# A gated unit in two column blocks of 512 instead of four of 256

## The chip, the cores and the metric

The kernel runs on one core of a Trainium2 chip. The core has five engines that work side by side, each on its own queue of instructions in program order: TensorE (PE, matrix products into PSUM), VectorE (DVE), ScalarE (ACT), GpSimd (POOL) and SyncE (SP, which here issues the DMAs). PSUM has eight banks of 512 fp32 columns. The metric is the device time of one execution in microseconds, from the chip.

## The reference

One layer of a hybrid backbone for 1,024 latent tokens of width 1,024 with 256 context tokens. Its mixer is a bidirectional S5 scan, then GELU, then a gated unit, then a residual; a SwiGLU FFN with 2,816 hidden channels and a final norm follow. The part the change touches:

```
g = gelu(y)                                  # (1024 tokens, 1024 channels)
y = g * sigmoid(g @ w_glu + b_glu)           # w_glu is 1024 x 1024
x = x + gate_mix * y                         # gate from the adaLN row
h = rms_norm(x) * (1 + scale) + shift        # input of the FFN
x = x + gate_ffn * swiglu(h, w1, w3, w2)
```

## The kernel before

All products must keep fp32 accuracy. A matrix is split in a high part `h`, rounded to the fast fp32r format, and a low part `l`, the rest; a product is three matmuls, h·wH + h·wL + l·wH. ACT or DVE makes the high part (a copy that rounds), POOL or DVE the low part (a subtraction).

The program is one order written by hand (a manual schedule): each engine runs its instructions in the order of the text, and waits only for data and for buffers. Up to the gated unit this order stands in two strings of codes, `PROG1` and `PROG2`, which `run` reads. The codes of the end of `PROG2`:

- `Q`, `H`: state products and GELU of channel block k (eight blocks of 128 channels)
- `I`, `J`: for tokens of the first half, transpose block k on PE and copy it as the high part (ACT), then make the low part (DVE); `GH[0]` holds both. `GH[1]` is for the second half
- `w`, `l`: load pieces of `w_glu` (raw fp32) into the buffers `wr0` and `wraw`; `b` loads the bias
- `W`, `V`: split weights into high and low parts. `V` first takes over the region `ra`, which held the scan's states
- `g`: the first matmuls of the gated unit, for those channel blocks that are ready. `g03` is token tile 0 up to block 3
- `x`: gate (multiply by the adaLN row) four blocks of one token tile on POOL

A *unit* `(cq, s)` is column block `cq` of `w_glu` for token tile `s` (eight tiles of 128 tokens). `glu_unit` issues its matmuls (`glu_mm`, lines L1092 to L1094), then on DVE the bias add, on ACT the sigmoid, on DVE the product and the add of the residual row `xs` (which is read from DRAM again, four rows of 512 KB at L1110), and on ACT a square with row sums for the norm (L1129). Between these it takes one step of each generator handed to it.

Before, `w_glu` is cut in four column blocks of 256, so there are 32 units of 24 matmuls. Two loops run them. The first loop runs the four blocks for token tiles 0 to 3. Its first eight units also turn the second half's channel blocks (`gt_steps`: four transposes, ACT copy, DVE subtraction). Weight blocks 2 and 3 are split inside this loop. The second loop runs token tiles 4 to 7, sixteen units numbered `u`. Beside them it makes the FFN's input for tiles that are done: `rms_steps` (a row sum and a chain of some twelve tiny DVE operations, L1152 and on), `h2s_steps` (POOL scales both halves of a tile, issued at the last step of a unit), and `h2t_steps` (four transposes a half, scale and shift on ACT for the first half and DVE for the second, ACT copy, subtraction on POOL for the first half and DVE for the second). One half is turned in each unit. At unit 12 the first FFN weights are split (`op_split`, four ACT casts and four POOL subtractions), and after unit 15 the up projection (`up_plain`, L1281 to L1283) starts. It turns the last tile after 36 of its matmuls.

PSUM tiles of both loops come from a pool of eight banks (`pe8`), each handed out again in the order in which they came free.

Of the kernel before, what the change touches and what calls it, by code (L numbers as in the profile page):

```python
# [10 lines left out]
F32 = mybir.dt.float32  # L11
# [6 lines left out]
P = 128  # L18
D = 1024
# [13 lines left out]
PROG2 = ("T12 T13 T14 T15 Z0 N0 Z1 Z2 D0 Z3 N1 D1 Z4 H0 H1 N2 D2 H2 w0 w1 l1 N3 Z5 D3 H3 N4 D4 z6 z7 I0 J0 I1 J1 H4 N5 D5 I2 J2 H5 I3 J3 W0 W1 x0 x1 x2 x3"  # L33
         " Q6 H6 I4 J4 Q7 b0 I5 J5 H7 g03 g13 I6 J6 g23 g05 g15 I7 J7 V1 w20 w21 g26 x10 x11 x12 x13")
LOG2E = 1.4426950408889634
LN2H = 0.693359375
LN2L = -2.12194440e-4
# [5 lines left out]
def s5_ffn_kernel(tc, a, out):  # L43
# [3 lines left out]
    with ctx:  # L47
# [906 lines left out]
        def run(prog):  # L954


            for w in prog.split():
# [7 lines left out]
                elif op == "L":  # L965
                    cs_load(i, S)
                elif op == "G":
                    cs_sign(i)
                elif op == "B":
                    bb_put(1, bb_turn(1))  # L970
                    bb_put(0, bb_turn(0))
                elif op == "C":
                    q, part = divmod(i, 10)
                    for f in cl_ops(q, part, cts[q][part], HOW[q][part]):
                        f()
                elif op == "F":
                    fill(*divmod(i, 10), *((RW, 0) if i >= 30 else (RC[3], 12)))
                elif op == "T":
                    toeplitz(i)
                elif op == "R":  # L980
                    turned(i, 0, HSe[i], S)
                elif op == "Z":
                    turned(i, 1, HSl[i], ENG[ZEN[i]])
                elif op == "z":
                    turned(i, 2, HSq[i], ENG[ZEN[i]])
                elif op == "P":
                    inner[i] = x_mm(i, pw)
                    states_mm(i, inner[i], 0, HSe[i], False)
                elif op == "Q":
                    inner[i] = x_mm(i, pe8)  # L990
                    states_all(i, inner[i], HSq[i])
                elif op == "Y":
                    S.copy(yview(i // 2, i % 2), inner[i // 2][i % 2])
                elif op == "N":
                    late[i] = [pe8([4, T, HC]) for _ in range(2)]
                    states_mm(i, late[i], 1, HSl[i], True)
                elif op == "D":
                    for gp, po in enumerate(late[i]):
                        tt(yview(i, gp), po, yview(i, gp), ADD)
                elif op == "H":  # L1000
                    if i in late:
                        S.activation(Y[:, i], Y[:, i], AF.Gelu_apprx_tanh)
                    else:
                        for gp in range(2):
                            S.activation(yview(i, gp), inner[i][gp], AF.Gelu_apprx_tanh)
                elif op == "I":
                    if GH[0] is None:
                        GH[0] = tuple(view(region(t, 16, R32), 0, [4, 8, P]) for t in ("c1", "c0"))
                    late[i] = gt_hi(i, 0)
                elif op == "J":  # L1010
                    gt_lo(i, 0, late[i])
                elif op == "W":
                    if not WR:
                        W0.append(region("c2", 16, R32))
                        WR.append((view(W0[0], 0, [8 * 256]), view(W0[0], 8, [8 * 256])))
                    v = slice(1024 * i, 1024 * i + 1024)
                    split(wr0[i], (WR[0][0][:, v], WR[0][1][:, v]), E, V)
                elif op == "w":
                    cq, h = divmod(i, 10)
                    SY.dma_start(wr0[h], a["w_glu"][cq][:, 1024 * h:1024 * h + 1024])  # L1020
                elif op == "b":
                    SY.dma_start(bglu, a["b_glu"].to_broadcast([P, D]))
                elif op == "l":
                    load_glu(i)
# [12 lines left out]
        late, W0, WR, PZ, GH, GR = {}, [], [], {}, [None, None], []  # L1037
        wr0 = [view(RXa, 4, [1024]), view(RW, 0, [1024])]
        bglu = view(RU, 32, [D])
        wraw = view(RXc, 0, [2048])  # L1040

        def load_glu(cq):
            SY.dma_start(wraw, a["w_glu"][cq])
# [39 lines left out]
        def glu_mm(cq, s, ks):  # L1083

            wH, wL = (w.rearrange("p (k n) -> p k n", k=8) for w in WR[cq])
            h_, l_ = gh_(s)
            new = (cq, s) not in PZ
            if new:
                PZ[cq, s] = [pe8([256]), 0]
            pz, n = PZ[cq, s]  # L1090
            for k in ks[n:]:
                PE.matmul(pz, h_[:, k], wH[:, k], start=n == 0, stop=False)  # L1092
                PE.matmul(pz, h_[:, k], wL[:, k], start=False, stop=False)
                PE.matmul(pz, l_[:, k], wH[:, k], start=False, stop=n == 7)  # L1094
                n += 1
            PZ[cq, s][1] = n
            return pz

        HOW = [[{"P": PE, "Y": SY, "E": E, "V": V}[c] for c in h] for h in HOWS.split()]
# [8 lines left out]
        xs = [view(X1, 4 * i, [D]) for i in range(4)]  # L1108
        for s in range(4):
            SY.dma_start(xs[s], xr[:, s])  # L1110
        TT = [[view(GR, 32 + 16 * i + 8 * j, [4, 4, P]) for j in range(2)] for i in range(3)]
        def glu_unit(cq, s, *others):

            def step():
                for g in others:
                    next(g, None)

            cs_ = slice(cq * 256, cq * 256 + 256)
            pz = glu_mm(cq, s, range(8))
            step()  # L1120
            tt(pz, pz, bglu[:, cs_], ADD)
            S.activation(pz, pz, AF.Sigmoid)  # L1122
            step()
            y = Y[:, 2 * cq:2 * cq + 2, s]
            o = pz.rearrange("p (k n) -> p k n", k=2)
            tt(o, o, y, MUL)
            tt(y, o, xs[s % 4][:, cs_].rearrange("p (k n) -> p k n", k=2), ADD)
            step()
            S.activation(o, y, AF.Square, accum_out=ssq[:, s, cq:cq + 1])  # L1129
            step()  # L1130
# [18 lines left out]
        def rms_steps(s0, s1):  # L1149
            sl = slice(s0, s1)  # L1150
            yield
            V.tensor_reduce(ss2[:, sl], ssq[:, sl], AX.X, ADD)  # L1152
            rsqrt(rt[:, sl], ss2[:, sl], rtt[:, sl])
            yield

# [40 lines left out]
            SY.dma_start(wraw[:, 512 * a0:512 * a1], a["w13"][ft].rearrange("p w k n -> p (w k n)")[:, 512 * a0:512 * a1])  # L1196
# [68 lines left out]
        GB = [[view(g, kb + 4 * i, [D]) for i in range(4)] for g, kb in ((G2, 0), (GR, 32))]  # L1265

        def gb(ft):
            return GB[ft == NFT - 1]
# [445 lines left out]
def layouts(i):  # L1714
# [30 lines left out]
    a["w_glu"] = c(f["s5_w_glu"][0].reshape(8, P, 4, 256).transpose(2, 1, 0, 3).reshape(4, P, 2048))  # L1745
# [22 lines left out]
```

## Time and profile before

| | us |
|---|---|
| median of 3 runs | 1016.01 (1014.42 to 1016.13) |
| the profiled execution | 1015.21 |
| its span, first to last instruction | 1013.4 |
| first gated-unit matmul to first up matmul | 258.79 to 361.32 |

In the rows of the profile, a line of the table by stretches gives for each engine the busy us and, in brackets, how many instructions it ran in the stretch, then the clock granted to PE (1.00 is full) and the DMA share and GB/s. In a row in order of time stand start, duration, engine, line, operation, output <- inputs, shape, and in brackets the idle time before it with what ended it; x4 means four instructions in one row. In a group, `| 1.2, 1218 |` are busy us and mean ns of one. Matmuls are pipelined, so their pace is read from start to start and not from their duration. L77 is the helper that issues every two-operand elementwise instruction. Buffer names: `pe` is PSUM of this stage, `ru` holds the residual stream, `rxa`, `rw` and `rxc` are the raw buffers `wr0` and `wraw` point into, `c` and `ra` hold split operands.

### The profile page before, as it was taken

The page shows a single profiled execution, that of the slowest core. Times are in us where ns is not written, and L with a number is a line of the kernel's source. Part 1 is how long each engine was busy: PE and PEld are TensorE (multiplying, and loading weights), DVE is VectorE, ACT ScalarE, POOL GpSimd, SP SyncE. Part 2 cuts the span into 40 slices and gives each one's busy share as a digit, 9 for nine tenths or more (in the row PEclk, how much of TensorE's full clock was granted, in tenths as well). Part 3 has the DMA queues.
Part 4 walks back from the last instruction along what each step waited for, and adds up shares of the span by engine and source line. Part 5 has one row for each costly group of instructions (what it writes and reads, how often), then busy time and mean ns, then how long its engine had stood idle before and what let it go on. Part 6 is the DMA issues. An engine that isn't in the chain of part 4 may idle for free. (4 is left out here: it accounts for less than half of the span.)

```text
span 1013.4 us, 18560 instructions
## 1 busy us (share of the span) xinstructions
PE 959.4 (95%) x6988; PEld 772.1 (76%) x6988; DVE 780.4 (77%) x1638; ACT 438.9 (43%) x860; POOL 763.4 (75%) x590
## 2 busy tenths in 40 slices
PE   5988798779999999999999999999999999999996
PEld 1466523679999988778888888888888888888885
DVE  7989699996356867877958677686959677686987
ACT  5478622335444663443343343324343343324337
POOL 5799998994672448979785878777786878777764
PEclk9999999999999999999999999999999999999998
DMA  9765997334512021011212111121212111121205
GB/s 336 280 135 95 280 346 247 95 84 138 188 46 80 2 104 63 27 44 46 73 42 83 42 52 42 50 66 53 73 42 83 43 52 43 46 70 53 73 22 166
DMA packets 48546, 98.96 MB, mean 98 GB/s; under 512 B 4284, under 2 KB 18876, under 8 KB 47176
## 3 DMA queue, kind: packets, MB, share of 16 engines
q1 hardware_dynamic: 43272, 86.64, 26.0%
q0 software_dynamic: 2016, 7.34, 3.9%
q10 hardware_dynamic: 3168, 3.79, 1.1%
q8 instruction: 55, 0.90, 0.4%
q14 instruction: 35, 0.29, 0.1%
HBM read 84.25 MB, written 6.17 MB: 89 GB/s over the span
## 5 line engine op out<-in xcount | busy, mean ns | idle before, releaser
L77 POOL TENSOR_TENSOR c<-rxc,c 128x512 fp32r<-128x512 f32 x128 | 166.6, 1315 | 53.5 <-ACT c L1222 52.7
L1282 PE MATMUL ut<-ra,c 128*128 128x512 f32 x400 | 155.7, 389 | 1.2 <-DVE ra L77 1.2
L1281 PE MATMUL ut<-ra,c 128*128 128x512 f32 x400 | 155.7, 389 | 0.2 <-ACT ra L1222 0.2
L1283 PE MATMUL ut<-ra,c 128*128 128x512 f32 x400 | 155.6, 389 | 0.0
L1222 ACT CAST c<-rxc 128x512 fp32r<-128x512 f32 x128 | 79.1, 622 | 147.0 <-PE xt L1576 53.3
L1576 PE MATMUL xt<-c,c 128*128 128x512 f32 x540 | 129.7, 389 | 0.0
L1576 PEld LDWEIGHTS xt<-c,c 128*128 128x128 f32 x540 | 101.4, 188 | 21.0
L77 DVE TENSOR_TENSOR ru<-ru,xt 128x1024 f32<-128x1024 f32 x90 | 107.3, 1215 | 10.9 <-PE xt L1576 7.9
L77 DVE TENSOR_TENSOR ru<-ut,ru 128x512 f32<-128x512 f32 x98 | 67.2, 686 | 43.0 <-PE ut L1283 37.6
L1282 PEld LDWEIGHTS ut<-ra,c 128*128 128x128 f32 x400 | 75.1, 188 | 17.0 <-POOL rxc L77 1.5
L1281 PEld LDWEIGHTS ut<-ra,c 128*128 128x128 f32 x400 | 75.1, 188 | 16.1 <-ACT ra L1222 0.6
L1283 PEld LDWEIGHTS ut<-ra,c 128*128 128x128 f32 x400 | 75.1, 188 | 15.5
L77 POOL TENSOR_TENSOR c<-rw,c 128x512 fp32r<-128x512 f32 (+1 forms) x29 | 41.1, 1417 | 37.8 <-ACT c L1222 37.8
L77 POOL TENSOR_TENSOR c<-ru,c 128x512 fp32r<-128x512 f32 (+1 forms) x39 | 57.1, 1465 | 10.1 <-ACT c L1222 5.7
L1281 PE MATMUL ut<-c,c 128*128 128x512 f32 x160 | 62.3, 390 | 0.8 <-DVE rxa L77 0.8
L77 POOL TENSOR_TENSOR rxc<-rxc 128x512 f32<-128x512 f32 x40 | 61.4, 1535 | 1.6
L1282 PE MATMUL ut<-c,c 128*128 128x512 f32 x160 | 62.2, 389 | 0.0
L1283 PE MATMUL ut<-c,c 128*128 128x512 f32 x160 | 62.2, 389 | 0.0
L1576 PE MATMUL ut<-c,c 128*128 128x512 f32 x216 | 51.9, 389 | 0.0
L584 PE MATMUL pv<-ru,c 128*64 128x160 f32 x512 | 45.0, 316 | 5.6 <-ACT rxa L388 1.8
L77 DVE TENSOR_TENSOR pe<-pe,ru 128x256 f32<-128x256 f32 x64 | 27.4, 429 | 29.5 <-ACT pe L1122 17.4
L77 DVE TENSOR_TENSOR ru<-ru,ut 128x512 f32<-128x512 f32 x76 | 47.3, 680 | 0.3
(444 smaller groups left out, 2569.1 us busy)
## 6 DMA issues: line engine op xcount, KB each, us to landing
c<-in_ada_w SPq DMA_DIRECT2D x46, 256.0 KB
rxc<-in_w SPq DMA_DIRECT2D x38, 256.0 KB
rxc<-in_w SPq DMA_DIRECT2D x19, 512.0 KB
ru<-in_w SPq DMA_DIRECT2D x11, 512.0 KB
rw<-in_w SPq DMA_DIRECT2D x11, 512.0 KB
ra<-in_ada_w SPq DMA_DIRECT2D x10, 512.0 KB
ra<-in_ada_w SPq DMA_DIRECT2D x18, 256.0 KB
ru<-in_xT SPq DMA_DIRECT2D x4, 1024.0 KB
```

What stands on the lines that cost most here:

```text
L77: eng.tensor_tensor(out=o, in0=x, in1=y, op=op)
L584: PE.matmul(pv[64 * (i % 2):64 * (i % 2) + 64, ri, c0:c0 + 160], w[:, i, 64 * ri:64 * ri + 64], U[:, 8 * b + 4 * j + i], start=True, stop= ...
L1222: S.copy(o[0], x)
L1281: PE.matmul(pu, wh, bh, start=start, stop=False)
L1282: PE.matmul(pu, wh, bl, start=False, stop=False)
L1283: PE.matmul(pu, wl, bh, start=False, stop=stop)
L1576: PE.matmul(pd, w[:, cs_], b, start=j in (1, 2, 4) and n == 0, stop=n == 2, skip_group_check=j not in (1, 2, 4))
```

## The change

`w_glu` is cut in two column blocks of 512, so there are 16 units of 24 matmuls, each filling a whole PSUM bank. The order of work around them changes with it:

- The first block arrives in four raw quarters (`w0 w1` and the first `l1`), of which DVE makes the high parts (`W0` to `W3`). The low parts are made in `V1`, two on POOL and two on DVE, since they lie in region `ra`. Until then `g` codes multiply by the high weights alone (`glu_h`: h·wH and l·wH). Units (0, 0) to (0, 2) then start with nothing left but their eight products with the low weights.
- The second block's raw quarters (`w20 w21` and the second `l1`) are loaded into the same four buffers behind `V1`, and before the residual rows `xs` on SP's queue. They are split after units (0, 0) and (0, 1), two quarters each, high on ACT and low on POOL.
- The gates `x10` to `x13` move from the end of `PROG2` to after unit (0, 2).
- In the first loop all eight units turn a channel block; in the second, eight units each turn both halves of a tile. The norms run at u = 0, 4 and 6, and `op_split` at u = 6.

```diff
-PROG2 = ("T12 ... I3 J3 W0 W1 x0 x1 x2 x3"
-         " Q6 H6 I4 J4 Q7 b0 I5 J5 H7 g03 g13 I6 J6 g23 g05 g15 I7 J7 V1 w20 w21 g26 x10 x11 x12 x13")
+PROG2 = ("T12 ... I3 J3 W0 W1 W2 W3 x0 x1 x2 x3"
+         " Q6 H6 I4 J4 Q7 b0 I5 J5 H7 g03 g13 I6 J6 g23 g05 g15 I7 J7 V1 w20 w21 l1 g26")
...
                 elif op == "W":
-                    if not WR:
+                    if not W0:
                         W0.append(region("c2", 16, R32))
-                        WR.append((view(W0[0], 0, [8 * 256]), view(W0[0], 8, [8 * 256])))
-                    v = slice(1024 * i, 1024 * i + 1024)
-                    split(wr0[i], (WR[0][0][:, v], WR[0][1][:, v]), E, V)
+                        late["wh"] = view(W0[0], 0, [8, 512])
+                    V.tensor_copy(view(W0[0], 4 * i, [1024]), wr0[i])
...
                 elif op == "V":
                     GR.append(region("ra", 80.5, R32))
-                    GH[1] = (view(GR[0], 0, [4, 8, P]), view(GR[0], 16, [4, 8, P]))
-                    WR.extend((view(GR[0], kb, [8 * 256]), view(GR[0], kb + 8, [8 * 256])) for kb in (32, 48, 64))
-                    split(wraw, WR[i], E)
+                    GH[1] = (view(GR[0], 16, [4, 8, P]), view(GR[0], 32, [4, 8, P]))
+                    WR.append((view(W0[0], 0, [8 * 512]), view(GR[0], 0, [8 * 512])))
+                    WR.append((view(GR[0], 48, [8 * 512]), view(GR[0], 64, [8 * 512])))
+                    for j in range(4):
+                        v = slice(1024 * j, 1024 * j + 1024)
+                        tt(WR[0][1][:, v], wr0[j], WR[0][0][:, v].bitcast(F32), SUB, (E, V)[j % 2])
                 elif op == "g":
-                    glu_mm(0, i // 10, range(i % 10 + 1))
+                    glu_h(i // 10, i % 10 + 1)
...
+        wr0 = [view(RXa, 4, [1024]), view(RW, 0, [1024]), wraw[:, 0:1024], wraw[:, 1024:2048]]
...
+        def glu_h(s, n):
+            wH = late["wh"]
+            h_, l_ = gh_(s)
+            if s not in PZ:
+                PZ[s] = [pe8([512]), 0]
+            pz, n0 = PZ[s]
+            for k in range(n0, n):
+                PE.matmul(pz, h_[:, k], wH[:, k], start=k == 0, stop=False)
+                PE.matmul(pz, l_[:, k], wH[:, k], start=False, stop=False)
+            PZ[s][1] = max(n, n0)
...
+            if cq == 0 and s < 4:
+                glu_h(s, 8)
+                pz = PZ[s][0]
+                for k in range(8):
+                    PE.matmul(pz, h_[:, k], wL[:, k], start=False, stop=k == 7)
+                return pz
...
-        load_glu(3)
-        for cq in range(4):
+        for s in range(3):
+            glu_h(s, 8)
+        for cq in range(2):
             for s in range(4):
                 k = 4 * cq + s
-                glu_unit(cq, s, *([gt_steps(k)] if cq < 2 else []))
-                if cq < 2 and s % 2:
+                glu_unit(cq, s, gt_steps(k))
+                if s % 2:
                     gate(slice(4, 8), slice(k - 1, k + 1))
-                if cq == 0 and s in (1, 2):
-                    v = slice(1024 * s - 1024, 1024 * s)
-                    split(wr0[s - 1], (WR[2][0][:, v], WR[2][1][:, v]), E)
-                if cq == 1 and s == 1:
-                    split(wraw, WR[3], E)
-                    raw13(0)
-                if cq == 3:
+                if cq == 0 and s < 2:
+                    for j in (2 * s, 2 * s + 1):
+                        v = slice(1024 * j, 1024 * j + 1024)
+                        split(wr0[j], (WR[1][0][:, v], WR[1][1][:, v]), E)
+                    if s:
+                        raw13(0)
+                if k == 2:
+                    for j in range(4):
+                        gate(j, slice(4, 8))
+                if cq:
                     SY.dma_start(xs[s], xr[:, s + 4])
...
-        RMS = {0: (0, 4), 8: (4, 6), 12: (6, 7)}
-        for u in range(16):
-            s, cq = 4 + u // 4, u % 4
+        RMS = {0: (0, 4), 4: (4, 6), 6: (6, 7)}
+        for u in range(8):
+            s, cq = 4 + u // 2, u % 2
             gens = []
-            if u >= 2:
-                j, kk = (u - 2) // 2, u % 2
-                gens.append(h2t_steps(j, pe8, tba[j % 2], kk))
+            if u:
+                gens.extend(h2t_steps(u - 1, pe8, tba[(u - 1) % 2], kk) for kk in range(2))
             if u in RMS:
                 gens.append(rms_steps(*RMS[u]))
-            if u % 2 == 0 and u < 14:
-                gens.append(h2s_steps(u // 2, tba[u // 2 % 2]))
+            if u < 7:
+                gens.append(h2s_steps(u, tba[u % 2]))
             glu_unit(cq, s, *gens)
-            if u == 12:
+            if u == 6:
                 for j in range(4):
                     op_split(0, j, raw[:, j])
                 raw13(1)
```

The rest follows from it: slices of 512 columns and four channel blocks in `glu_unit`, two instead of four row sums a tile, other offsets in region `ra` for later buffers, and the layout of `w_glu` in DRAM.

More of the change, by code (lines that the diff above doesn't have):

```diff
@@ L1030, in run, with load_glu @@
                     GR.append(region("ra", 80.5, R32))
-                    GH[1] = (view(GR[0], 0, [4, 8, P]), view(GR[0], 16, [4, 8, P]))
-                    WR.extend((view(GR[0], kb, [8 * 256]), view(GR[0], kb + 8, [8 * 256])) for kb in (32, 48, 64))
-                    split(wraw, WR[i], E)
+                    GH[1] = (view(GR[0], 16, [4, 8, P]), view(GR[0], 32, [4, 8, P]))
[4 more added lines that the diff above has]
+                        tt(WR[0][1][:, v], wr0[j], WR[0][0][:, v].bitcast(F32), SUB, (E, V)[j % 2])
                 elif op == "g":
-                    glu_mm(0, i // 10, range(i % 10 + 1))
-        late, W0, WR, PZ, GH, GR = {}, [], [], {}, [None, None], []
-        wr0 = [view(RXa, 4, [1024]), view(RW, 0, [1024])]
+                    glu_h(i // 10, i % 10 + 1)
+        late, W0, WR, PZ, GH, GR, LG = {}, [], [], {}, [None, None], [], []
         bglu = view(RU, 32, [D])
         wraw = view(RXc, 0, [2048])
-        def load_glu(cq):
-            SY.dma_start(wraw, a["w_glu"][cq])
+        wr0 = [view(RXa, 4, [1024]), view(RW, 0, [1024]), wraw[:, 0:1024], wraw[:, 1024:2048]]
+        def load_glu():
+            n = len(LG)
+            LG.append(n)
+            SY.dma_start(wraw, a["w_glu"][n][:, 2048:4096])
         def pe8(shape, tag="e", bufs=8):
@@ L1081, in gate, with glu_mm @@
             tt(y, y, bc(g, 2, n) if n else g, MUL, E)
-        def glu_mm(cq, s, ks):
+        def glu_h(s, n):
[8 more added lines that the diff above has]
+            PZ[s][1] = max(n, n0)
+        def glu_mm(cq, s):
             wH, wL = (w.rearrange("p (k n) -> p k n", k=8) for w in WR[cq])
             h_, l_ = gh_(s)
[L1087 to L1092, printed above, removed]
+            if cq == 0 and s < 4:
[4 more added lines that the diff above has]
+                return pz
+            pz = pe8([512])
+            for k in range(8):
+                PE.matmul(pz, h_[:, k], wH[:, k], start=k == 0, stop=False)
                 PE.matmul(pz, h_[:, k], wL[:, k], start=False, stop=False)
-                PE.matmul(pz, l_[:, k], wH[:, k], start=False, stop=n == 7)
-                n += 1
-            PZ[cq, s][1] = n
+                PE.matmul(pz, l_[:, k], wH[:, k], start=False, stop=k == 7)
             return pz
@@ L1110, in s5_ffn_kernel @@
             SY.dma_start(xs[s], xr[:, s])
-        TT = [[view(GR, 32 + 16 * i + 8 * j, [4, 4, P]) for j in range(2)] for i in range(3)]
+        TT = [[view(GR, kb + 8 * j, [4, 4, P]) for j in range(2)] for kb in (0, 48, 64)]
         def glu_unit(cq, s, *others):
@@ L1116, in step @@
                     next(g, None)
-            cs_ = slice(cq * 256, cq * 256 + 256)
-            pz = glu_mm(cq, s, range(8))
+            cs_ = slice(cq * 512, cq * 512 + 512)
+            pz = glu_mm(cq, s)
             step()
@@ L1123, in glu_unit @@
             step()
-            y = Y[:, 2 * cq:2 * cq + 2, s]
-            o = pz.rearrange("p (k n) -> p k n", k=2)
+            y = Y[:, 4 * cq:4 * cq + 4, s]
+            o = pz.rearrange("p (k n) -> p k n", k=4)
             tt(o, o, y, MUL)
-            tt(y, o, xs[s % 4][:, cs_].rearrange("p (k n) -> p k n", k=2), ADD)
+            tt(y, o, xs[s % 4][:, cs_].rearrange("p (k n) -> p k n", k=4), ADD)
             step()
@@ L1264, in s5_ffn_kernel @@
         G2 = region("c3", 16, R32)
-        GB = [[view(g, kb + 4 * i, [D]) for i in range(4)] for g, kb in ((G2, 0), (GR, 32))]
+        GB = [[view(g, kb + 4 * i, [D]) for i in range(4)] for g, kb in ((G2, 0), (GR, 0))]
         def gb(ft):
```

10 lines of the change are left out of this document (5 added, 5 removed).

## The prediction

> **What bounds the kernel now.** I read the page's busy shares first, then the table by stretches, then the instructions in order of time for each engine, the waits of the DMA queue, and the groups by shape for prices.
>
> ```profile
> PE 959.4 (95%) x6988; PEld 772.1 (76%) x6988; DVE 780.4 (77%) x1638; ACT 438.9 (43%) x860; POOL 763.4 (75%) x590
> 260.00:280.00 20.00, 20.00 (x172) 20.00 (x172) 8.20 (x18) 11.43 (x22) 11.84 (x6) 1.00 0.45 157
> 340.00:360.00 20.00, 20.00 (x171) 20.00 (x170) 16.33 (x52) 13.56 (x38) 12.11 (x11) 1.00 0.01 2
> 500.00:600.00 100.00, 100.00 (x443) 82.81 (x442) 70.64 (x85) 38.66 (x67) 80.73 (x61) 1.00 0.14 45
> ```
>
> TensorE (PE) is full in the gated unit (second and third row) and after it (fourth), at full clock (1.00). So a microsecond that PE saves or waits in the gated unit moves the end by the same amount. The stage runs from its first matmul to the first of the up projection:
>
> ```profile
> 258.79 0.36 PE L1092 MATMUL pe<-c,c 128*128 128x256 f32 x1
> 361.32 0.48 PE L1281 MATMUL pu<-c,c 128*128 128x512 f32 x1
> 289.81 0.28 PE L1092 MATMUL pe<-ra,c 128*128 128x256 f32 x1
> 299.17 0.28 PE L1092 MATMUL pe<-ra,c 128*128 128x256 f32 x1
> 376.68 0.39 PE L1282 MATMUL pu<-ra,c 128*128 128x512 f32 x1
> 379.40 0.39 PE L1282 MATMUL pu<-ra,c 128*128 128x512 f32 x1
> 317.89 0.60 PE L1172 MATMUL pe<-r,rxa 128*128 128x128 f32 x4
> 318.25 0.36 PE L1092 MATMUL pe<-ra 128*128 128x256 f32 x1
> 369.60 1.03 PE L1172 MATMUL pd<-r,rxa 128*128 128x128 f32 x8
> 370.39 0.48 PE L1281 MATMUL pu<-c,c 128*128 128x512 f32 x1
> 370.70 0.40 PE L1282 MATMUL pu<-c,c 128*128 128x512 f32 x1
> ```
>
> The stage lasts 102.5 us. 78 matmuls of 256 columns lie between the third and fourth row: 0.120 us each. Of 512 columns, 12 lie between the fifth and sixth: 0.2267. Four transposes hold PE for 0.36, eight for 0.79, and the first matmul behind takes 0.08 more (0.31 for 0.227).
>
> **The change part by part.** *Matmuls.* 768 at 0.120 become 384 at 0.2267: 92.2 less 87.1 is 5.1 us saved, all on PE. In the second loop fourteen interruptions of 0.36+0.08 become seven of 0.79+0.08: 6.2 against 6.1, nothing. If nobody is late: -5.1.
>
> That DVE and ACT also issue half as many instructions in the stage changes no time of its own, since neither is what PE waits for now; where their wider instructions lengthen a chain, it is counted below.
>
> [...]
>
> *Second block's weights.* These rows price the first loop:
>
> ```profile
> 265.05 0.60 PE L1051 MATMUL pe<-r,ru 128*128 128x128 f32 x4
> 265.69 0.59 ACT L1053 CAST c<-pe 128x512 fp32r<-128x512 f32 x1 [2.73 <-PE pe L1051]
> 266.31 0.69 DVE L77 TENSOR_TENSOR c<-pe,c 128x512 fp32r<-128x512 f32 x1 [2.62 <-ACT c L1053]
> 253.54 0.69 DVE L77 TENSOR_TENSOR c<-pe,c 128x512 fp32r<-128x512 f32 x1 [4.31 <-ACT c L1053]
> L77 DVE TENSOR_TENSOR ru<-ru,rxa 128x1024 f32<-128x1024 f32 x1 | 1.2, 1218 | 0.0
> 268.59 1.28 ACT L1122 ACT_TABLE_LOAD   x1
> 273.73 0.39 ACT L1129 ACTIVATE pe<-ru 128x256 f32<-128x256 f32 x1 [1.11 <-DVE ru L77]
> 274.14 1.04 ACT L1068 CAST ra<-rxa 128x1024 fp32r<-128x1024 f32 x1
> 280.10 2.40 POOL L77 TENSOR_TENSOR ra<-rxa,ra 128x1024 fp32r<-128x1024 f32 x1
> 294.13 2.39 POOL L77 TENSOR_TENSOR ru<-ru,rxa 128x1024 f32<-128x1024 f32 x1
> 253.88 0.36 SPq L1020 DMA_DIRECT2D rw<-in_w_glu  x1
> 258.55 2.66 SPq L1110 DMA_DIRECT2D c<-in_x  x4
> 272.80 0.33 SPq L1043 DMA_DIRECT2D rxc<-in_w_glu  x1
> SPq L1196 <- DMA rxc<-in_w_glu: 4.8, 1, 4.8
> 260.00:265.00 5.00, 5.00 (x44) 5.00 (x44) 1.07 (x2) 1.23 (x3) 0.00 (x0) 1.00 0.91 317
> ```
>
> PE's new clock, from 258.79: 16 high matmuls, I6, 16 more, I7, then 16 (g26 and the completion) end at 270.6; eight low ones end unit (0,0) at 272.4. Units (0,1) and (0,2) follow with eight each, (0,3) with 24, all with transposes; unit (1,0) starts at 283.1 and would want its last low weights, as its 20th matmul, at 287.5.
>
> V's work hides: POOL's two subtractions run when the region is free (258.4) and end near 263; DVE's two stand behind J7. I7 is at 266.6, its copy 0.64 and J7 1.26 behind (265.05 to 266.31), so J7 ends 268.5 and DVE's two, 1.22 each, 269.7 and 270.9; PE wants the last at 272. The two extra high copies (W2, W3) cost DVE at most two passes of 1.22 in its 4.31 us gap; two POOL passes there go. Both: nothing.
>
> But the loads w20, w21 and l1 now wait for those subtractions, and in SP's queue the four x rows stand behind them. Before, w21 went at 253.88 and x at 258.55. After, w21 goes at 269.8, l1 at 271.0. A 1 MB load lands 5.1 us after its issue began (0.33+4.8), so l1 at 276.1. The first x row, 512 KB, follows at the 317 GB/s of the last row (x itself was moving then): 1.65 more, 277.8. Unit (0,0): ACT copies its transposes by 273.6 (0.64 behind PE and 0.59 long), loads the table (1.28, to 274.9), sigmoid to 275.5, DVE's product to 276.2; the x add waits for 277.9, the square runs 278.7 to 279.4 (0.41 for 256 columns, plus 0.25 for 256 more, the step from 0.37 to 0.62 in the rows below). Only then does ACT, which works in program order, copy the first quarter of the second block (1.04), to 280.4. POOL has the four subtractions and one gate of the same size between: five of 2.40, to 292.4. PE wants that at 287.5: it stalls 4.9 in unit (1,0), in pieces, as each quarter of the weights comes late (the second quarter is already 0.5 late, the third takes most). Behind the waiting x add DVE holds the low half of the transposes and the next unit's bias add; PE needs neither before 283.1, when it takes the PSUM bank that unit (0,0) gave up at 279.4. Ends: 3.3 if the x row is not late (1.7 sooner), 6.5 if it is a further 1.7 later. Gates x10 to x13, moved behind this on POOL, end near 297.4; only DVE's products wait for them, and PSUM has banks to spare. The first FFN load on SP waits for POOL's fourth subtraction, at 292.4, about when it did before; it is used 50 us later.
>
> *Second loop.* Each unit now does both transposed halves of one token tile, in half the units. The rows of one unit:
>
> ```profile
> 318.09 0.43 DVE L77 TENSOR_TENSOR pe<-pe,ru 128x256 f32<-128x256 f32 x1 [0.16 <-PE pe L1094]
> 318.56 0.37 ACT L1122 ACTIVATE pe<-pe 128x256 f32<-128x256 f32 x1
> 318.84 1.50 ACT L1181 ACTIVATE rxa<-pe,r 128x128 f32<-128x128 f32 x4
> 320.37 0.62 ACT L1183 CAST c<-rxa 128x512 fp32r<-128x512 f32 x1
> 321.12 1.29 POOL L77 TENSOR_TENSOR c<-rxa,c 128x512 fp32r<-128x512 f32 x1 [3.71 <-issue]
> 322.36 2.04 POOL L77 TENSOR_TENSOR rxa<-ru,r 128x512 f32<-128x512 f32 x2
> 321.84 1.78 DVE L86 TENSOR_SCALAR pe<-pe,r 128x128 f32<-128x128 f32 x4
> 338.51 0.15 DVE L1152 TENSOR_REDUCE r<-r 128x2 f32<-128x8 f32 x1
> 340.96 0.43 DVE L77 TENSOR_TENSOR pe<-pe,ru 128x256 f32<-128x256 f32 x1
> 357.71 5.04 POOL L77 TENSOR_TENSOR c<-rxc,c 128x512 fp32r<-128x512 f32 x4
> ```
>
> From the end of a unit's matmuls (317.89) to the end of POOL's two scalings (324.40) is 6.51; the bias add and the sigmoid, 512 wide, add 0.25 each: 7.0. PE comes back after 0.79+0.08+24x0.2267 = 6.31 and wants the second half 0.36 later, at 6.67; with 0.1 for the hand-over it waits 0.43. That wait moves the next unit, so every second one pays: 0.43 at u2 and u4. Where the norm runs (u4 and u6), DVE does the four scalings of the transposed half (1.0 to 2.8) and then the norm's 2.45 before POOL may start: 5.4 plus 2.04 and hand-overs, 7.6, a wait of 0.95 at u5 and u7, and 0.2 at u6: together 2.9. Ends: 1.1 with the chain 0.4 shorter, 4.4 with it 0.4 longer.
>
> Unit u0, with the first norm and no transposes, gives no wait: bias add to 0.9, norm to 3.4, both scalings to 5.6; PE wants the halves at 5.5 and 5.9, and the first is there at 4.6.
>
> *Start of the up projection.* Its first low operand comes from POOL behind u6's scalings and square: cast near 8.2, subtraction 1.26 (a quarter of 5.04), 9.6 after u6's matmuls; PE wants it at 8.8 by the waits above. 0.95; ends 0 and 1.9 (PE arriving 0.95 sooner). The last tile's scaling, on DVE behind u7's square, which stands behind ACT's four casts, ends about 10.8 after u7's matmuls; PE wants it behind 36 matmuls of the up projection, at 10.9: nothing, with no cover left. The weights for it (the second FFN load) go out as before, behind the casts.
>
> Sum: -5.1 + 4.9 + 2.9 + 0.95 = +3.7 us. The profiled execution took 1015.21 (span 1013.4 and 1.8 around it), 0.8 below the median of 1016.01; 1015.2 + 3.7 = **1018.9**. What a measurement of this kernel can tell from no change is about 0.2%, 2 us.
>
> **The rivals.**
> A, the forecast: its ends give 1014.5 to 1022.9.
> B, only the weights are late. For it: POOL in the second loop idles 3.71 us before its subtraction, and 0.4 off the chain removes most waits. Against: the same order of work holds. PE then reaches the up projection sooner and waits 1.9 there: -5.1+4.9+1.9 = 1016.9.
> C, the weights are in time, the second loop stalls. For it: POOL is free from 263 on. Against: ACT's order and five POOL passes. -5.1+2.9+0.95: 1014.0; with the low end 1.1, 1012.2.
> D, the other side: POOL's passes are much shorter than shown, since DVE works less beside them. Its price: five passes at the block change and 1.29+2.04 per unit; from about 1.65 us for 1024 columns instead of 2.40 (five times 0.75 and two more in the second loop off +3.7) it is 2 us faster, and with nothing left waiting 1010.1. Against: 2.40, 2.39 and 1.26 repeat wherever the neighbours differ.
> [...]
>
> **How the numbers follow.** A 0.52, B 0.20, C 0.10, D 0.12, E 0.06. A's low end (0.06) and most of B and C are within 2 us: same 0.28. D and the edge of C: faster 0.14. The rest of A, E and the upper part of B: slower 0.58. The range goes from C's low end, 1012.2, to A's high end and E, 1023.0; most of D and half of E are left out, under 0.2.
>
> **What would show it.** Right: matmuls 0.227 apart; four x loads issued after 271; five POOL passes without a gap from about 280.5 to 292.4, and a matmul of unit (1,0) waiting for POOL on ra; transposes of u2, u4, u5, u7 waiting for POOL on rxa; the first up matmuls waiting for POOL on c. Wrong: unit (1,0) in one piece, or ACT's four 1024-wide copies done before 278. The forecast falls if x lands early and POOL starts by 276, or if the chain of a unit is under 6.6 us.

## The result, and the profile after

| | before | after |
|---|---|---|
| median of the runs shown, us | 1016.07 (1014.42 to 1016.73) | 1024.96 (1023.16 to 1025.56) |
| the profiled execution, us | 1015.21 | 1023.16 |
| its span, us | 1013.4 | 1021.4 |
| first gated-unit matmul to first up matmul, us | 102.53 | 109.07 |

The ratio after to before is 1.0087, 95% interval 1.007 to 1.0104: slower by 0.9%. The forecast was 1018.9. Its direction held, but the loss is 8.0 us between the profiled executions and 8.9 between the medians, not 3.7.

The first six rows are PE's in order of time, of the profile after: the start of the stage, of unit (1,0), the transposes behind that unit, the unit behind it with its own transposes, and the start of the up projection. Behind them stand the rows of SP and DVE around the residual rows `x`, and POOL's last two passes for the second block.

```profile
259.18 0.47 PE L1095 MATMUL pe<-c,c 128*128 128x512 f32 x1
283.82 0.47 PE L1111 MATMUL pe<-ra,c 128*128 128x512 f32 x1
295.95 0.60 PE L1055 MATMUL pe<-r,ru 128*128 128x128 f32 x4
296.30 0.48 PE L1111 MATMUL pe<-ra,c 128*128 128x512 f32 x1
301.87 0.60 PE L1055 MATMUL pe<-r,ru 128*128 128x128 f32 x4
368.25 0.50 PE L1301 MATMUL pu<-c,c 128*128 128x512 f32 x1
...
271.77 3.21 SPq L1127 DMA_DIRECT2D c<-in_x  x4
279.86 0.69 DVE L77 TENSOR_TENSOR ru<-pe,c 128x512 f32<-128x512 f32 x1 [2.87 <-DMA c<-in_x]
289.41 4.68 POOL L77 TENSOR_TENSOR ra<-rxc,ra 128x1024 fp32r<-128x1024 f32 x2
```

The stage is 6.54 us longer. Unit (1,0), from its first matmul to the transposes that follow it, takes 12.13 us (283.82 to 295.95). The unit behind it, which waits for nothing, takes 5.57 (296.30 to 301.87). So the block change costs 6.56. The x rows leave SP at 271.77, and DVE stands idle 2.87 us for the first of them. POOL's last pass ends at 294.09, and the unit 1.9 us behind it.

The three longest of PE's waits from 238 to 400 us, by the profile after (us in total, times, longest us):

```profile
PE pe L1112 <- POOL ra L77: 4.2, 3, 3.0
PE pe L1189 <- POOL rxa L77: 2.5, 4, 0.9
PE pu L1303 <- POOL c L77: 0.6, 1, 0.6
```

The three places that the forecast named are the three rows. Unit (1,0) waits 4.2 us but loses 6.56. Most of the other 2.3 lies in the clock granted to PE (the number behind POOL's bracket) in that unit:

```profile
290.30:291.80 1.50, 0.00 (x0) 0.00 (x0) 1.50 (x3) 0.76 (x3) 1.50 (x2) 0.95 0.00 0
291.80:292.80 1.00, 0.98 (x2) 0.83 (x3) 0.35 (x1) 0.97 (x2) 1.00 (x1) 0.50 0.00 0
294.80:295.40 0.60, 0.60 (x3) 0.46 (x3) 0.09 (x1) 0.32 (x2) 0.60 (x2) 0.78 1.21 164
```

At the end of the 3.0 us wait the clock falls to 0.50 and stays there until about 295.06 (0.78 is 0.26 us at 0.50 and the rest at 1.00); by the 0.95 it fell at about 291.65, so it was at half for 3.4 us. The matmuls behind the wait start 0.43 apart instead of 0.227. PE works from 291.82 on, so 3.24 us at half pace lose 1.6; the remaining 0.7 stands at the edges of the three waits, where the matmul behind each takes 0.34 to the next start instead of 0.23. How much of the 1.6 the wait for POOL's last pass would have taken anyway is settled by the last experiment.

Of the second loop, the first four rows are the starts of units u2 and u5 to u7, the next ones the DVE and POOL rows about the norm of u4, the last is of the norm of u6:

```profile
325.86 0.48 PE L1111 MATMUL pe<-c,ra 128*128 128x512 f32 x1
345.58 0.47 PE L1111 MATMUL pe<-ra 128*128 128x512 f32 x1
353.64 0.48 PE L1111 MATMUL pe<-c,ra 128*128 128x512 f32 x1
360.18 0.48 PE L1111 MATMUL pe<-ra 128*128 128x512 f32 x1
...
348.18 1.29 POOL L77 TENSOR_TENSOR c<-rxa,c 128x512 fp32r<-128x512 f32 x1 [3.07 <-ACT c L1200]
348.35 1.14 DVE L77 TENSOR_TENSOR r<-r 128x2 f32<-128x2 f32 x1
349.92 0.16 DVE L77 TENSOR_TENSOR r<-r 128x2 f32<-128x2 f32 x1
351.14 2.04 POOL L77 TENSOR_TENSOR rxa<-ru,r 128x512 f32<-128x512 f32 x2 [1.67 <-DVE r L80]
363.10 1.33 DVE L80 SCALAR_TENSOR_TENSOR r<-r 128x1 f32<-128x1 f32 x2
```

A unit without waits takes some 6.35 here. u5 takes 8.06 (345.58 to 353.64) and u7 8.07 (360.18 to 368.25): 1.7 us lost in each. One operation of u4's norm, on two numbers a partition, lasts 1.14, where the same form a little later takes 0.16; u6's norm has two that take 1.33 together. The long one ends when POOL's subtraction beside it ends: 348.35 + 1.14 = 349.49, and 348.18 + 1.29 = 349.47. POOL's scalings wait for the norm.

### The profile page after: what moved, and what is told of

It reads as the page before. It is cut to its first block, busy times and chain, and to the rows that moved or that the text cites. A ratio compares the mean times of both kernels' runs of the same rounds, so it can differ in the third digit from the quotient of the medians.

```text
span 1021.4 us, 17681 instructions
## 1 busy us (share of the span) xinstructions
PE 957.6 (94%) x6604; PEld 751.1 (74%) x6604; DVE 781.1 (76%) x1594; ACT 431.2 (42%) x812; POOL 760.0 (74%) x590
## 5 line engine op out<-in xcount | busy, mean ns | idle before, releaser
L77 DVE TENSOR_TENSOR pe<-pe,ru 128x512 f32<-128x512 f32 x32 | 22.3, 697 | 32.3 <-PE pe L1113 18.4
```

What stands on the lines that cost most here:

```text
L77: eng.tensor_tensor(out=o, in0=x, in1=y, op=op)
```

## The experiments

Of the theory, each term was tried alone: the block change (weights, and what holds them back), the second loop's order, the width, and the two things of the profile after that the forecast had not foreseen, PE at half clock and the stretched norm.

**The residual rows first.** The x rows are loaded ahead of the second block's weights:

```diff
-run(PROG2)
-for s in range(4): SY.dma_start(xs[s], xr[:, s])
+run(PROG2[:cut])            # cut stands before " w20"
+for s in range(4): SY.dma_start(xs[s], xr[:, s])
+run(PROG2[cut:])
```

> The changed kernel with one thing moved: the four loads of the residual rows go out before the loads of the second weight block, so they no longer stand behind those on SP. Theory (the late x row starts the second block's split late): the product of unit (0,0) is done at 277.0 and the x add need not wait until 279.9, so ACT's copies and POOL's five passes move 2.9 us ahead and end near 291.2; unit (1,0) ends near 292.4 instead of 295.9, and the kernel is 3 to 3.5 us faster than the changed one (ratio to before near 1.0055). Rival (POOL's five passes alone set the end of unit (1,0), whenever x lands): under 1 us.

Measured: 1020.77, ratio 1.0038 (1.0022 to 1.0055); the profiled span is 3.1 us shorter than after's, and by the ratios the gain is 5.0. POOL starts the second block at 279.35, where after it was 282.39, and PE has one wait in unit (1,0) instead of three. The two rows in order of time are POOL's first subtraction and PE's wait:

```profile
279.35 2.40 POOL L77 TENSOR_TENSOR ra<-rxa,ra 128x1024 fp32r<-128x1024 f32 x1 [15.69 <-ACT ra L1072]
288.84 0.50 PE L1112 MATMUL pe<-ra,c 128*128 128x512 f32 x1 [2.02 <-POOL ra L77]
```

Two stretches behind that wait, with the clock:

```profile
288.80:290.00 1.20, 1.16 (x4) 0.98 (x5) 0.48 (x2) 0.92 (x2) 1.20 (x1) 0.76 0.00 0
292.60:293.20 0.60, 0.60 (x4) 0.45 (x3) 0.00 (x0) 0.00 (x0) 0.60 (x1) 0.79 0.59 205
```

So the x rows' place in SP's queue delayed POOL's passes by 3 us. The clock falls behind a wait of 2.02 too, here 0.6 us after PE had gone on (0.76 over 1.2 us is 0.58 at half), and again for 3.4 us: 0.79 is 0.25 of the last stretch at half, to 292.85. Unit (1,0) takes 9.59 (283.60 to 293.19), 4.0 more than a clean one: twice the wait.

**No second block.** Units (1,0) to (1,3) use the first block's weights; the second block's split goes on, but tiles 0 to 3 do not use it.

```diff
-wH, wL = (... for w in WR[cq])
+wH, wL = (... for w in WR[cq if s >= 4 else 0])
```

> The changed kernel, but the second column block of token tiles 0 to 3 is multiplied with the first block's weights, so that PE waits for no split there; the split itself, its loads and all other work stay where they are. Theory (the block change costs all that unit (1,0) took over a clean unit, 12.1 against 5.6 us): 6.5 us faster than the changed kernel, ratio to before near 1.002. Rival (only the three waits that the profile names count, 4.2 us, and the matmuls at half pace behind the longest wait are no part of it): 4.2 us faster, 1.0045. Rival (the wait comes back later, at PSUM banks or the gates): under 2 us.

Measured: 1017.1, ratio 1.0006 (0.9987 to 1.0024). PE's rows of the stage's start, unit (1,0), its end, and the first up matmul:

```profile
258.73 0.47 PE L1095 MATMUL pe<-c,c 128*128 128x512 f32 x1
283.37 0.47 PE L1111 MATMUL pe<-c,c 128*128 128x512 f32 x1
288.93 0.60 PE L1055 MATMUL pe<-r,ru 128*128 128x128 f32 x4
361.27 0.50 PE L1301 MATMUL pu<-c,c 128*128 128x512 f32 x1
```

The unit is 5.56 long and the stage 102.54, 6.5 less than after's 109.07: the late weights cost 6.5 by the trace. By the ratios they cost 0.0081, 8.2 us; what varies from run to run (the last experiment) is the likely rest. The rival of 4.2 us, the named waits alone, is out by both.

**The norm alone on DVE's time.** In u4 and u6 DVE itself makes the first half's low part, so POOL makes no pass during the norm:

```diff
-tt(..., SUB, V if kk else E)
+tt(..., SUB, V if kk or s in (3, 5) else E)
```

> The changed kernel, with the low half of the first transposed half subtracted on DVE instead of POOL in the two units where a norm runs (u4 and u6). Theory (a tiny DVE operation of the norm, 1.14 and 1.33 us instead of 0.16 and 0.35, was held until POOL's subtraction ended, and the scaling stands behind the norm): the norm takes 2.45 again, and the waits at u5 and u7 fall from 1.7 to about 0.8 each: 1.5 to 2 us faster, ratio to before near 1.007. Rival (the scaling waits for POOL's own order, not for the norm): the tiny operation is short but the time stays within 0.5 us.

Measured: 1025.49, ratio 1.0078 (1.005 to 1.0105): no gain that can be told from after's 1.0087.

```profile
350.80 0.16 DVE L77 TENSOR_TENSOR r<-r 128x2 f32<-128x2 f32 x1
352.67 2.04 POOL L77 TENSOR_TENSOR rxa<-ru,r 128x512 f32<-128x512 f32 x2 [5.11 <-DVE r L80]
353.77 1.48 DVE L77 TENSOR_TENSOR c<-rxa,c 128x512 fp32r<-128x512 f32 x1
```

The small operation is back to 0.16, as the theory says. u5 takes 7.15 (348.02 to 355.17) instead of 8.06, and u7 7.09 (363.05 to 370.14) instead of 8.07: the stretch alone is worth 0.9 to 1.0 in each. But the subtraction that DVE took over lies beside POOL's scaling and lasts 1.48; the next bias add on DVE stands behind it, and u6 becomes 7.88 (355.17 to 363.05) instead of 6.54. That step of the theory held, and most of the gain was lost again in u6.

**The scaling before the rest.** The generators of the second loop are stepped in the order norm, scaling, transposed halves, so on DVE the norm stands ahead of the four scale-and-shifts and on POOL the scalings ahead of the subtraction:

```diff
-gens = [h2t_steps x2, rms_steps, h2s_steps]
+gens = [rms_steps, h2s_steps, h2t_steps x2]
```

> The changed kernel, with the order of the steps in the second loop turned: norm, then scaling, then the transposed halves, so that POOL scales before it subtracts and DVE's norm stands before its four scale-and-shift operations. Theory (PE's waits in the second loop come from POOL's scaling behind the chain sigmoid, four ACT operations, copy, subtraction): all waits at u2 to u7 go, 4.3 us, but PE arrives sooner at the up projection and waits there 1.9 to 2.9 instead of 0.9: 2.3 to 3.3 us faster, ratio to before near 1.006. Rival (the waits come from PSUM banks or from DVE's own load): they stay, under 1 us.

Measured: 1022.22, ratio 1.0062 (1.0039 to 1.0084). The rows are the starts of u7 and of the up projection:

```profile
359.54 0.48 PE L1111 MATMUL pe<-ra 128*128 128x512 f32 x1
366.35 0.50 PE L1301 MATMUL pu<-c,c 128*128 128x512 f32 x1 [0.22 <-ACT c L1243]
```

The longest of PE's three waits from 300 to 400 us (one is the 0.22 of the row above, one, 0.2, the profile before has too):

```profile
PE pu L1303 <- POOL c L77: 0.6, 1, 0.6
```

No matmul waits for POOL on rxa any more. u0 to the up projection takes 50.30 (316.05 to 366.35) against 54.19 after (314.06 to 368.25): 3.9 us. The stage of this profile is only 1.95 shorter (107.12 against 109.07): unit (1,0) took 13.46 instead of 12.13, and the clock, here at half for 6.8 us, slowed the start of the next unit by another 0.6.

**Norm first, subtraction still ahead of the scaling.** This parts the stretched norm from the order on POOL:

```diff
-gens = [h2t_steps x2, rms_steps, h2s_steps]
+gens = [rms_steps, h2t_steps x2, h2s_steps]
```

> The changed kernel with only the norm moved ahead of DVE's four scale-and-shift operations in the units u4 and u6; POOL still subtracts before it scales. Theory (the two long waits are the norm's place on DVE, once behind those four and once held by POOL's subtraction): the norm is done before POOL starts to subtract, no tiny operation is stretched, u5 and u7 wait 0.35 like u2 and u4 instead of 1.7, 2.7 us less than the changed kernel beside it. Rival (POOL's subtraction and scaling set the waits of u5 and u7 whatever the norm does): under 1 us.

Measured: 1024.25, ratio 1.0079 (1.0065 to 1.0093), 2.75 below the median of the changed kernel beside it (1027.0, in the last experiment). The two intervals overlap, so the rows have to carry it: one of the norm, and the starts of u2 and of the up projection.

```profile
350.88 0.16 DVE L77 TENSOR_TENSOR r<-r 128x2 f32<-128x2 f32 x1
330.69 0.48 PE L1111 MATMUL pe<-c,ra 128*128 128x512 f32 x1
369.92 0.50 PE L1301 MATMUL pu<-c,c 128*128 128x512 f32 x1
```

u2 to the up projection takes 39.23 (330.69 to 369.92) against 42.39 after (325.86 to 368.25): 3.2 us less, 2.7 expected. So the norm's place, behind DVE's scalings and beside POOL's subtraction, is most of the second loop's loss; POOL's order is the rest (3.9 with both). By the gains at u5 and u7 with the norm alone, some 1.9 of the 3.2 are the stretched operations and 1.3 the place behind the scalings; no run parts the two cleanly.

**The second block's weights early.** The x rows come first as above, and the second block is split in two steps: the high parts of two quarters on DVE ahead of unit (0,0), two on ACT behind it, with no gate of POOL between the four subtractions:

```diff
+for j in range(2): split2(j, V)           # before the first loop; low on POOL
...
-if cq == 0 and s < 2: split two quarters, high on ACT
+if k == 0:
+    for j in (2, 3): split2(j, S)
+    raw13(0)
```

> The changed kernel with the residual rows loaded first, and the second weight block split sooner: its first two quarters get their high part on DVE ahead of unit (0,0)'s bias add, the last two on ACT behind unit (0,0), all low parts on POOL without a gate between. Theory (the block change costs 6.5 us because ACT and POOL begin the split behind unit (0,0)'s chain and the x row): POOL ends the fourth part near 285, before PE asks for it at 288; unit (1,0) runs clean in 5.6 us and the kernel stands level with the one before, ratio 0.999 to 1.002. Rival (something else holds unit (1,0), or the gates pushed back on POOL now hold the later units): a ratio of 1.004 or more.

Measured: 1018.21, ratio 1.0004 (0.999 to 1.0018). PE's waits from 258 to 365 us:

```profile
PE pe L1191 <- POOL rxa L77: 2.5, 4, 0.9
PE pu L1310 <- POOL c L77: 0.6, 1, 0.6
```

Unit (1,0) as one stretch:

```profile
283.76:289.32 5.56, 5.56 (x28) 4.55 (x27) 4.09 (x7) 3.45 (x8) 5.56 (x4) 1.00 0.54 187
```

The block change is free: 5.56 for the unit at full clock, and the stage 102.51 (259.12 to 361.63), as with no second block at all. What is left over the width's gain is the second loop.

**Both cures.** Early weights, scaling first, and the first of `op_split`'s four parts right behind u6's matmuls:

```diff
 # e5 and the order norm, scaling, halves; then
+if u == 6: gens.insert(0, (op_split(0, j, raw[:, j]) for j in range(1)))
```

> As the last one, and also the second loop with norm and scaling ahead of the transposed halves, and the first FFN operand split right behind u6's matmuls. Theory (width saves about 4 to 5 us on PE and every wait found was one of order): all named waits go, and against the kernel before it is 3 to 4.5 us faster, ratio 0.9955 to 0.9975. Rival (taking the waits away only moves them to the up projection): a ratio of 0.999 or more.

Measured: 1012.34, ratio 0.9948 (0.9933 to 0.9963). It is faster than both kernels. PE's one wait from 258 to 400 us, and then the first and last row of the stage:

```profile
PE pu L1311 <- POOL ra L77: 0.2, 1, 0.2
```

```profile
261.96 0.47 PE L1095 MATMUL pe<-c,c 128*128 128x512 f32 x1
360.10 0.48 PE L1310 MATMUL pu<-c,c 128*128 128x512 f32 x1
```

The stage lasts 98.14 instead of before's 102.53, 4.4 less.

**The width alone.** The kernel with both cures, each matmul of 512 columns issued as two of 256 into the same bank:

```diff
-PE.matmul(pz, h_[:, k], wH[:, k], ...)              # and so for the two others
+for c in (slice(0, 256), slice(256, 512)):
+    PE.matmul(pz[:, c], h_[:, k], wH[:, k, c], ...)
```

> As the last one, but each matmul of 512 columns issued as two of 256 into the halves of the same bank, everything else the same: the width alone. Theory (pace by the rows of before, 0.120 for 256 and 0.227 for 512): 5.1 us slower than the last one. [...]

Measured: 1016.18, ratio 0.9998 (0.9979 to 1.0016).

```profile
259.08 0.36 PE L1096 MATMUL pe<-c,c 128*128 128x256 f32 x1
361.62 0.47 PE L1313 MATMUL pu<-c,c 128*128 128x512 f32 x1
```

The stage is 102.54, the time of before to 0.01, and 4.40 above the same order with 512 columns: the width is worth 4.4 us by the trace, 5.1 by the ratios (0.0050).

**PE kept busy in the wait.** Twelve matmuls into a spare bank, which nothing reads, are issued in unit (1,0) ahead of the third late quarter. It ran once, and then several times with the changed kernel itself beside it:

```diff
+if (cq, s, k) == (1, 0, 4):                  # junk is a bank of its own
+    for i in range(12): PE.matmul(junk, h_[:, 0], wH[:, 0], start=True, stop=True)
```

> The changed kernel with twelve idle matmuls of 512 columns into a spare bank put where unit (1,0) waits longest (before its third quarter of low weights), 2.7 us of work in a wait of 3.0. Theory (the matmuls behind that wait ran at 0.43 instead of 0.227 because PE had been idle): now they run at 0.227, and unit (1,0) ends about 0.6 us sooner, where POOL's fourth part sets it. Rival (the slow pace comes from reading weights that POOL is just writing, or with chance in time): the pace stays 0.43.

> The changed kernel itself again, as the measure for the two beside it. By its four earlier runs: ratio to before 1.007 to 1.010, and a profile that lies below its median, if in most runs the matmuls behind the long wait run at half pace for longer than in the profiled one.

> The kernel with twelve idle matmuls in unit (1,0)'s longest wait, now timed. Theory (half pace behind the idle wait costs 0.5 to 2 us by run, and is part of the changed kernel's loss): 1 to 2 us faster than the changed kernel beside it, with less spread. Rival (the half pace costs nothing because POOL sets the end of unit (1,0) anyway): within 0.5 us.

Measured: 1020.88 in the single run; in five runs 1023.23, ratio 1.0072 (1.0059 to 1.0085); the changed kernel beside it 1027.0, 1.0102 (1.0086 to 1.0117), 3.8 more by the medians and 3.1 by the ratios, where 1 to 2 were expected. Unit (1,0) of the busy kernel, from 288 on:

```profile
288.00:294.90 6.90, 5.88 (x25) 4.19 (x24) 4.58 (x7) 3.33 (x8) 6.90 (x5) 1.00 0.10 13
```

The clock stays at 1.00, the matmuls behind the waits are 0.23 apart, and the unit (283.26 to 294.93) ends 1.31 behind POOL's last pass (293.62) instead of 1.86. The rival, that the slow pace comes from reading weights which POOL is just writing, is out: POOL writes them here too. The same stretch of the changed kernel's second profile, from the end of its long wait:

```profile
295.72:300.58 4.86, 4.86 (x12) 3.67 (x13) 2.34 (x4) 1.69 (x4) 4.86 (x4) 0.50 0.33 93
300.58:302.00 1.42, 1.42 (x7) 1.33 (x6) 0.70 (x1) 0.33 (x1) 1.42 (x2) 0.56 0.95 404
```

And of that profile the x add and POOL's last passes:

```profile
283.79 0.69 DVE L77 TENSOR_TENSOR ru<-pe,c 128x512 f32<-128x512 f32 x1 [4.24 <-DMA c<-in_x]
293.32 4.67 POOL L77 TENSOR_TENSOR ra<-rxc,ra 128x1024 fp32r<-128x1024 f32 x2
```

Here the clock is at half until about 301.8, for 6.8 us, and the unit ends 2.6 behind POOL's last pass (297.99 to 300.58). The transposes and the first matmul behind it take 0.70 and 0.57 instead of 0.35 and 0.32. So half clock cost 0.55 us in the first profile of the changed kernel and about 1.9 in this one (1.28 and 0.6). The rest of this profile's longer unit (14.2 against 12.13) is the x row: DVE waited 4.24 for it instead of 2.87. Two things in the block change vary from run to run, then, the arrival of the x row and the length of the spell at half clock; they make the stage 2.7 longer in this profile (111.77 against 109.07). They are not all: the stage also starts 2.55 later here (261.73 against 259.18), and in the two profiles of the kernel kept busy at 256.69 and 258.62. Why is not shown, so what the medians differ by can't be shared out. Keeping PE busy takes away the half clock alone.

## Why the prediction was right or wrong

The direction, the three places and the releasers were right; the size was not. Term by term, in us:

| term | predicted | measured | shown by |
|---|---|---|---|
| matmuls of 512 | -5.1 | -4.4 | no-wait kernel and halves |
| second block's weights | +4.9 | +6.56 | unit (1,0); no second block, 6.5 |
| second loop's waits | +2.9 | +4.3 | units u2 to u7 over 6.35 each |
| start of the up projection | +0.95 | +0.92 | its first three matmuls, 1.70 instead of 0.78 |
| sum | +3.7 | +7.4 | |

The profiled executions differ by 8.0. Of the 0.6 that the sum leaves, 0.39 is there before the stage starts (259.18 against 258.79), less than that start moves between two executions of the changed kernel; the other 0.2 lies behind the stage and was not placed.

- *Matmuls.* The pace was right at 0.227. A clean unit takes 5.57, though, where 24 times 0.2267 and 0.08 are 5.52; a clean unit of the halves takes 5.84, which is 48 times 0.120 and 0.08. Sixteen times 0.27 is 4.3 of the 4.4. The saving was put 0.7 too high: a unit of 512 takes 0.05 more than its pace gives, sixteen times. E and the range's 1023.0 stand for a width that saves 1.0; no run shows that, and the halves showed 4.4 in its place.
- *Second block's weights: the term that failed most.* The chain was right to the link: x loads at 271.77, ACT behind the x add, five POOL passes of 2.4 without a gap. Two sizes were not. The x row was priced from the 1 MB load before it, at its arrival 277.8 (277.9 for the add); the add began at 279.86. With the stage's start 0.39 later, the row was 1.6 late, near the high end that the prediction kept (1.7). The forecast gave the first row the whole rate of 317 GB/s. The stretch from the first of the weight loads to the add, 270.13 to 279.86, ran at 297 GB/s, which makes 2.9 MB, and the two weight loads and the first row are 2.1 MB; so the later rows seem to have taken a share of the rate. That is an inference: no run loads the first row alone. POOL's passes ended at 294.09 instead of 292.4. And PE was taken to go on at full pace behind its wait; it went on at half. The missing 1.7 is worked out as follows: beside the common 0.39 the passes end 1.3 later than forecast and the unit starts 0.3 later, which makes late passes 1.0; the unit ends 1.86 behind the last pass instead of 1.1, which makes the other 0.75. The kernel with PE kept busy ends 1.31 behind it, so 0.55 of the 0.75 is the clock, and 0.2 the forecast's own tail.
- *Second loop.* The alternation was right: waits in every second unit and the larger ones at u5 and u7 (1.71 and 1.72, where 0.95 was forecast). The step that failed is "then the norm's 2.45": beside POOL's subtraction one of the norm's operations lasts until that pass ends (1.14 instead of 0.16), and the norm takes 3.43 in u4 (347.55 to 350.98) and 3.35 in u6 (362.16 to 365.51). The 2.45 was taken from a place in the trace before (338.51 to 340.96) where POOL ran nothing.
- *Start of the up projection.* The wait on c is 0.63 and its edges the rest of 0.92: the size was right. With no wait ahead of it (scaling first) the new waits there were 0.2 and 0.6, so rival B's 1.9 did not come.
- *Covered at nothing, and so it was:* V's work, the two more high copies, the moved gates; no wait of PE in the profile after names them.
- *Why the time left the range.* Its top was 1023.0, about A's high end (1022.9), 4.0 above the forecast, with every wait at its end. Block change and second loop came out nearly there (1.7 and 1.4 above), the matmuls saved 0.7 less, and 0.6 lay outside the sum: 1023.16 in the profiled execution. The median is 1.8 above that. The forecast had added its sum to a profiled execution that lay 0.8 below its own median; the rest goes with what varies from run to run and was not shared out.

Rival D did not come true (the passes are 2.38 to 2.39, the last two 4.68 together), nor B, nor C: early weights and scaling first, each tried without the other, show that both stretches stall, independent of each other.

## What to carry to other kernels

Wider matmuls paid most of what the pace of the neighbouring stage said (4.4 of 5.1 us), but halving the units halves the slack behind which the other engines hid, and each late operand is paid in full. When a step is moved ahead of a load in a queue, follow what stands behind it there (here x rows behind weights) to the engine that works in program order. Two microseconds of idle PE cost more than the wait here (2.02 of waiting made unit (1,0) 4.0 longer with the x rows first), so the wait and the pace behind it both belong in the sum.

## What the hardware showed that was not expected

*The clock fell behind waits of 2.0 to 3.0 us, for 3.4 or 6.8 us.* With such waits in unit (1,0) the granted clock was 0.50 for 3.4 us in three profiles (after, x first, norm alone) and for 6.8 in three others (scaling first, norm first, the changed kernel again). In the kernels without such a wait it was 1.00 in the whole stage, and with PE kept busy it was 1.00 from 280 to 296 us in the single run and from 288 to 294.9 in the profile of the five. Behind the stage it was 1.00 until the last 7 us of the kernel, before and after. Ahead of the stage it falls too: from 200 to 250 us its mean is 0.97 before and after, and 0.90 in the changed kernel again. In the profile after, the spells ahead of the stage start at 110.74, 124.40, 196.08 and 213.14 and the one in unit (1,0) at 291.65: 4, 21, 5 and 23 times 3.413 us apart. In the one before they start at 69.47, 110.43 and 199.17: 12 and 26 times 3.413. The table by stretches, cut in steps of 3.41 us at the start of the spell, shows what the spells go with. The first two lines are of the profile after, the last two of the changed kernel's second profile:

```profile
288.24:291.65 3.41, 0.57 (x3) 0.14 (x1) 2.09 (x4) 1.79 (x5) 3.41 (x2) 1.00 0.00 0
291.65:295.06 3.41, 3.24 (x8) 2.54 (x9) 2.49 (x4) 1.79 (x5) 3.41 (x3) 0.50 0.00 0
291.58:294.99 3.41, 1.15 (x5) 0.58 (x4) 1.51 (x3) 1.79 (x4) 3.41 (x2) 1.00 0.00 0
294.99:298.40 3.41, 2.68 (x6) 2.13 (x7) 2.66 (x5) 1.79 (x5) 3.41 (x3) 0.50 0.00 0
```

PE is busy for 0.57 of 3.41 us, and the clock is at half in the next 3.41; there PE is busy for 3.24, and the clock comes back. In the other profile 1.15 is followed by half clock, and 2.68 in the first such step by a second one. The six profiles split in this way: 0.4 to 1.4 us of work in the step ahead of every fall, 3.24 or more in the first step of the three short spells, 2.68 to 2.78 in that of the three long ones. From the start of the stage to 400 us no such step of the six with 2.09 or more of work was followed by a fall from 1.00, though waits of 1.88 and 0.70 lie in such steps (the changed kernel again); nothing between 1.4 and 2.09 was seen. That the place of a wait in these steps counts along with its length is an estimate from these rows; no run moves a wait alone. For one and the same kernel that place differed: 0.57 us of work in the step ahead of the fall in one execution, 1.15 in the other, and the spell was 3.4 us in the first and 6.8 in the second. What sets the clock is not shown.

*A tiny DVE operation lasted until a POOL pass ended.* In u4's norm 0.16 us became 1.14, ending within 0.02 us of POOL's subtraction (349.49 and 349.47). In u6's norm the first of the two operations that take 1.33 together has 1.14 of it, and ends at 364.24, where POOL's subtraction ends at 364.22. With the norm alone and with the norm first POOL runs no pass beside the norm of u4, and there u4's operation takes 0.16. So in these rows its time goes with the end of the pass beside it and not with its own size, one or two numbers a partition. Why it is held is not shown.
